# First stage of an encoder block in another order: one modulation summed on TensorE, two heads per output product

## The chip, the cores and the metric

The kernel runs on one core of one Trainium2 chip. The metric is the device time of one execution in microseconds (us), as the median of several runs. TensorE (PE in the profile) multiplies matrices and transposes through products with an identity; VectorE (DVE), ScalarE (ACT) and GpSimd (POOL) work on rows; SyncE (SP) issues the transfers. Each engine takes its own instructions strictly in order and waits on semaphores for the others.

## The reference

One encoder block on 512 tokens of 1024 channels, in float32. A mixing layer is followed by a layer of 16 experts.

```python
mod = silu(c) @ w_ada + b_ada
shift1, scale1, gate1, shift2, scale2, gate2 = split(mod, 6)
h = rms_norm(x, npm) * (1 + scale1) + shift1
q, k, v, zg = split(h @ w_in)               # 512, 128, 128, 1024 columns
attn = windowed_gqa(q, k, v, sink)          # 8 heads, 2 kv heads, band of +-128
u, vg = split(gelu(zg), 2)
gm = u * (W_s @ layer_norm(vg) + b_s)       # per chunk of 128 tokens, 8 groups
mix = concat([rms_norm(attn), rms_norm(gm)])
x = x + gate1 * rms_norm(mix @ w_out)
h2 = rms_norm(x, npf) * (1 + scale2) + shift2
y = experts(h2)       # each of 16 experts takes its best 64 tokens, SwiGLU, 2816 wide
x = x + gate2 * rms_norm(y)
```

## The kernel before

Two stages follow each other. The **first stage** is the mixing layer with the router; the **expert stage** streams the weights of 16 experts through 13 buffers of 1408 KB. The order in which the program writes its steps, and a scheduler that works at build time, fix the sequence on every engine; at run time nothing is reordered.

**Projection.** `SEQ` lists three kinds of step for the eight groups of 128 channels. `m` makes shift1 and scale1 of a group, `d` modulates the group (`modulate`, L332 to L334) into a high part `hh` and a low part `hl`, and `q` adds the group's products into q, k and v (`qkv`; every product is three, L346 to L348, with the weights split in parts `wh` and `wl`). A step `m` has two forms. For the groups in `MODPE` (0, 1, 2, 3, 5) TensorE sums 32 small products (`mod1_rows`, L293). For groups 4, 6 and 7 VectorE adds eight rows (`mod1_acc`, L315 and L317), and TensorE then sums over partitions (`mod1_cols`, L322).

**Gate units, up units.** Then come eight units `g` and eight units `u` of the gMLP's projection, 12 products each (`pg`, `pu`). For each unit GpSimd makes the low part of the weights (`wl`, L343). Into the gate units the kernel weaves the sums of gate1 and shift2 (`mod2(0)`, `mod2(1)`: eight VectorE instructions of 128x1024 on `racc` each, L553 and L555, with loads from `w_ada`); scale2 (`mod2(2)`, numbers in `M2`) and gate2 (`mod2(3)`, `M3`) lie in the attention steps. `mod2_cols` turns a finished sum into columns with TensorE (`pm`, then a transpose `pt`). `gate_norm` normalises one block of the gate values `vn`: statistics (L499), 1/sqrt, a scaling on VectorE (L505), and two products on GpSimd (L506, L507). Blocks 0 and 1 do so after the last units, blocks 2 and 3 in steps of the attention (`GN`).

**Attention steps.** A numbered loop of 26 steps follows. Step i makes the scores of one block and one pair of heads (`sp`, L430) and the softmax (L432 on), and two steps later transposes the probabilities (`ptr`, L454; copied to `pT`) and multiplies them with v (`po`, L462). Up units 4 to 7 are in steps 0 to 3. `todo` hangs the rest on step numbers: spatial gating, splitting the output weights (`wo`, `wz`, L654 and L657), the output projection (`py`), the residual (L698), the router's logits, and in step `RS` the ranks of the first three blocks (`rank_part`, L806). Step `GS` spreads gate2 over all partitions (L585).

**1/sqrt.** `rsqrt(dst, v, n)` guesses from the bits (L184), forms -v/2 (L186), and takes three Newton steps (L191 for n = 1, L193 and L194 for more, then L196). The norm of x is done in two calls, n = 3 and n = 1 (L258).

**Transfers.** All go out on SyncE's queue in program order. The expert weights are issued at L835, each into a buffer that an earlier tile has to leave.

Of the kernel before, what the change touches and what calls it, by code (L numbers as in the profile page):

```python
# [7 lines left out]
F32 = mybir.dt.float32  # L8
# [39 lines left out]
TINY = 2.0 ** -126  # L48


@with_exitstack
def encoder_block(ctx, tc, x, c, w_ada, b_ada, norm_pre_mix, norm_post_mix, w_in, sink, sgu_ln_g,
# [32 lines left out]
    # ---------------------------------------------------------------- loads  # L85
# [17 lines left out]
    # columns of w_ada for shift1, scale1 of 128 channels with the rows of w_in for q, k, v of these channels  # L103
# [18 lines left out]
    def more_loads():  # L122
# [15 lines left out]
        nc.sync.dma_start(lnb, sgu_ln_b.to_broadcast([P, DG]))  # L138
        wst = slot([NG, P], name="wst")
# [4 lines left out]
    # ---------------------------------------------------------------- constants  # L144
# [24 lines left out]
    def make_dist():  # L169
        """|distance|, or a huge number outside the window; keys in front of, of, behind the block"""  # L170
# [10 lines left out]
    def rsqrt(dst, v, n):  # L181
        """dst = 1/sqrt(v) for [P, n] f32, to f32's accuracy: a guess from the bits, then Newton."""
        i = rs.tile([P, n], I32, name="rs_i", tag=f"rs_i{min(n, 2)}", bufs=2 if n == 1 else 1)
        nc.vector.tensor_scalar(i, v.bitcast(I32), -0.5, float(0x5F3759DF), op0=OP.mult, op1=OP.add)  # L184
        h = rs.tile([P, n], F32, name="rs_h", tag=f"rs_h{min(n, 2)}", bufs=2 if n == 1 else 1)
        nc.vector.tensor_scalar(h, v, -0.5, None, op0=OP.mult)  # L186
        y = i.bitcast(F32)
        t = rs.tile([P, n], F32, name="rs_t", tag=f"rs_t{min(n, 2)}", bufs=2 if n == 1 else 1)
        for r in range(3):
# [5 lines left out]
            o = dst if r == 2 else rs.tile([P, n], F32, name="rs_y", tag=f"rs_y{min(n, 2)}")  # L195
            nc.vector.scalar_tensor_tensor(o, t, 1.5, y, op0=OP.add, op1=OP.mult)  # L196
            y = o
# [4 lines left out]
    def rms(src, n, junk, dst=None):  # L202
        """1/rms of the rows of src (one [P, n] or two halves of it)"""
        parts = src if isinstance(src, list) else [src]
        ss = rs.tile([P, len(parts)], F32, name="ss", tag=f"ss{len(parts)}")
        for i, p in enumerate(parts):
            sumsq(ss[:, i:i + 1], p, junk[:, :p.shape[1]])
        if len(parts) > 1:
            nc.vector.tensor_tensor(ss[:, 0:1], ss[:, 0:1], ss[:, 1:2], op=OP.add)
        v = rs.tile([P, 1], F32, name="vv")  # L210
        nc.vector.tensor_scalar(v, ss[:, 0:1], 1.0 / n, EPS, op0=OP.mult, op1=OP.add)
        r = rs.tile([P, 1], F32, name="rr", bufs=4) if dst is None else dst
        rsqrt(r, v, 1)
        return r

    # ---------------------------------------------------------------- parameters by column
# [20 lines left out]
    # ---------------------------------------------------------------- x: transposed; 1 / rms  # L237
# [18 lines left out]
    def x_rsqrt(b0, b1):  # L256
        v = ssx[:, b0:b1]
        nc.vector.tensor_scalar(v, v, 1.0 / D, EPS, op0=OP.mult, op1=OP.add)  # L258
# [8 lines left out]
    # ---------------------------------------------------------------- shift1, scale1; h  # L267
# [817 lines left out]
```

## Time and profile before

| | us |
|---|---|
| median of three runs | 1546.49 |
| lowest, highest | 1546.27, 1547.13 |
| span of the profiled execution | 1544.5 |
| TensorE busy | 1387.1 |
| VectorE busy | 429.7 |
| ScalarE busy | 188.9 |
| GpSimd busy | 116.0 |

The profile is one execution. Its span runs from the first to the last instruction; the page gives no other time of that execution, and the median is 2.0 us above the span. [...] The first sixth of the span and the rest have different limits, so a share over the whole says nothing on either of them.

### The profile page before, as it was taken

To read this page: it belongs to the slowest core of one execution; us is meant where nothing else is said; L and a number is where in the kernel's file an instruction comes from. 1 tells how busy PE (TensorE), PEld (TensorE's weight loads), DVE (VectorE), ACT (ScalarE), POOL (GpSimd) and SP (SyncE) were. 2 spreads that over 40 slices of the span, in tenths; PEclk is the share of its full clock that TensorE was granted. 3 is DMA by queue.
4 is the path that set the end of the run, shared out by engine and by line. 5 is a ranking of instruction groups with operands and counts; after the bars stand their busy time and mean duration, and the time that the engine had idled before them with its cause. 6 is when DMAs were issued, how large, how long until landed. Compare 5 with 4: busy or idle time off the path is not lost.

```text
span 1544.5 us, 17570 instructions
## 1 busy us (share of the span) xinstructions
PE 1387.1 (90%) x7282; PEld 619.8 (40%) x7282; DVE 429.7 (28%) x1087; ACT 188.9 (12%) x404; POOL 116.0 (8%) x144
## 2 busy tenths in 40 slices
PE   7888998999999998998898998989898989898986
PEld 5665665343444433333333333324242423333323
DVE  5789857112112120212112111112020303020104
ACT  3336433000010000000100000000000000000001
POOL 2457310000000000000000000000000000000002
PEclk9998999999999999999999999999999999999998
DMA  9776608999999999999999999999999999999995
GB/s 316 275 252 181 241 6 334 415 411 428 429 429 429 429 429 428 429 428 429 429 428 429 429 429 429 429 428 429 429 428 429 429 429 429 428 429 429 429 396 202
DMA packets 92711, 596.86 MB, mean 386 GB/s; under 512 B 8692, under 2 KB 31960, under 8 KB 44760
## 3 DMA queue, kind: packets, MB, share of 16 engines
q1 hardware_dynamic: 92632, 595.74, 93.3%
q8 instruction: 57, 0.93, 0.2%
q14 instruction: 22, 0.18, 0.0%
HBM read 593.62 MB, written 2.10 MB: 386 GB/s over the span
## 4 chain that ended last, share of the span: by engine, by line
DMA 60%; PE 28%; DVE 8%; issue 1%; ACT 1%; POOL 1%; SPq 0%; DVEq 0%; ACTq 0%; POOLq 0%
DMA w<-in_w_down_dram 23%; DMA w<-in_w_up_dram 19%; DMA w<-in_w_gate_dram 18%; PE pf L949 11%; PE pd L991 4%; PE px L888 1%; PE pys L1001 1%; PE py L348 1%; PE py L346 1%; PE po L462 1%; PE py L347 1%; DVE ex L851 1%; PE pd L1031 1%; DVE racc L555 1%; DVE acc L317 1%
## 5 line engine op out<-in xcount | busy, mean ns | idle before, releaser
L949 PE MATMUL pf<-w,ex 128*64 128x512 f32 (+1 forms) x3072 | 638.0, 561 | 42.0 <-DMA w<-in_w_up_dram 40.6
L949 PEld LDWEIGHTS pf<-w,ex 128*64 128x64 f32 x3072 | 215.0, 137 | 433.2 <-issue 326.2
L991 PE MATMUL pd<-w,ex 128*64 128x512 f32 (+1 forms) x1440 | 319.3, 563 | 33.7 <-DMA w<-in_w_down_dram 33.7
L991 PEld LDWEIGHTS pd<-w,ex 128*64 128x64 f32 x1440 | 109.9, 136 | 231.7 <-issue 126.0
L967 DVE TENSOR_TENSOR ex<-pf,ex 128x512 f32<-128x512 f32 (+1 forms) x48 | 30.4, 647 | 362.3 <-PE pf L949 362.0
L995 DVE TENSOR_SCALAR ex<-pd,gc 128x512 f32<-128x512 f32 x15 | 11.3, 751 | 377.6 <-PE pd L991 377.6
L907 POOL COPY ex<-ex 128x512 f32<-128x512 f32 x16 | 9.8, 613 | 1138.2 <-DVE ex L905 1058.0
L888 PE MATMUL px<-x_sb,ex 128*64 128x256 f32 x512 | 71.0, 386 | 8.6 <-DVE ex L864 7.4
L919 ACT ACTIVATE ex<-pot 128x512 f32<-128x512 f32 x16 | 9.6, 597 | 544.6 <-PE pot L917 544.6
L1007 DVE TENSOR_TENSOR y<-pys,y 128x512 f32<-128x512 f32 x112 | 68.2, 681 | 17.0 <-PE pys L1001 17.0
L974 ACT ACTIVATE ex<-pht 128x512 f32<-128x512 f32 (+1 forms) x48 | 23.5, 559 | 374.6 <-PE pht L973 374.6
L1001 PE MATMUL pys<-ex 64*128 64x512 f32 x240 | 55.6, 602 | 12.7 <-DVE ex L995 12.7
L900 DVE TENSOR_SCALAR ex<-pxt,mods 128x64 f32<-128x64 f32 x128 | 34.9, 337 | 92.0 <-PE pxt L895 92.0
L888 PEld LDWEIGHTS px<-x_sb,ex 128*64 128x64 f32 x512 | 41.3, 136 | 38.3 <-DVE ex L864 18.8
L851 DVE SCALAR_TENSOR_TENSOR ex<-rt,afs,before 128x512 f32<-128x512 f32 (+2 forms) x65 | 46.8, 719 | 12.3 <-PE rt L858 12.3
L913 DVE COPY gc<-pgc 128x1 f32<-128x1 f32 x16 | 2.5, 158 | 152.6 <-PE pgc L910 152.6
L555 DVE SCALAR_TENSOR_TENSOR racc<-ada,cs,racc 128x1024 f32<-128x1024 f32 x28 | 42.6, 1521 | 0.2
L959 ACT ACTIVATE ex<-pf 128x512 f32<-128x512 f32 (+1 forms) x48 | 26.9, 561 | 121.2 <-PE pf L949 120.4
L1001 PEld LDWEIGHTS pys<-ex 64*128 64x128 f32 x240 | 21.9, 186 | 47.1 <-DVE ex L995 25.9
L973 PE MATMUL pht<-ident,ex 128*128 128x128 f32 x176 | 25.7, 295 | 12.1 <-DVE ex L967 12.1
L973 PEld LDWEIGHTS pht<-ident,ex 128*128 128x128 f32 x176 | 22.7, 213 | 22.7 <-DVE ex L967 22.7
L890 ACT ACTIVATE ex<-px 128x256 f32<-128x256 f32 x32 | 12.3, 383 | 125.7 <-PE px L888 125.6
(254 smaller groups left out, 1086.3 us busy)
## 6 DMA issues: line engine op xcount, KB each, us to landing
w<-in_w_gate_dram SPq DMA_DIRECT2D x128, 1408.0 KB, 26.8
w<-in_w_up_dram SPq DMA_DIRECT2D x126, 1408.0 KB, 26.8
w<-in_w_down_dram SPq DMA_DIRECT2D x120, 1408.0 KB, 26.8
ada<-in_w_ada_dram SPq DMA_DIRECT2D x16, 1024.0 KB, 6.5
w<-in_w_down_dram SPq DMA_DIRECT2D x18, 512.0 KB, 9.6
wq<-in_w_ada_dram SPq DMA_DIRECT2D x16, 512.0 KB, 5.9
wi<-in_w_in_dram SPq DMA_DIRECT2D x4, 1024.0 KB, 5.2
wq<-in_w_in_dram SPq DMA_DIRECT2D x8, 384.0 KB, 6.2
```

The costliest lines, as they stand in the source:

```text
L555: nc.vector.scalar_tensor_tensor(acc[i], t[:, r], cs[:, k:k + 1], acc[i], op0=OP.mult, op1=OP.add)
L851: nc.vector.scalar_tensor_tensor(junk[:, :c1 - c0], p[:, c0:c1], afs[:, b, e:e + 1], before[:, o + c0:o + c1], op0=OP.subtract, op1=OP.is_ ...
L888: nc.tensor.matmul(px[i][h * CAP:(h + 1) * CAP, :256], ohr[:, b], x_sb[:, b, c0:c0 + 256], start=(b == 0), stop=(b == NB - 1))
L900: nc.vector.tensor_scalar(xs[:, k], pt[:, c0:c0 + CAP], s2[:, k:k + 1], sh2[:, k:k + 1], op0=OP.mult, op1=OP.add)
L949: nc.tensor.matmul(pb[n][h * 64:(h + 1) * 64, :NW[n]], XS[e][:, k], t, start=(i == 0), stop=(i == KD - 1))
L959: nc.scalar.activation(hid[:, n * 512:n * 512 + NW[n]], pg[n][:, :NW[n]], AF.Silu)
L967: nc.vector.tensor_tensor(hs, pu[n][:, :NW[n]], hs, op=OP.mult)
L973: nc.tensor.transpose(p[:, j * P:(j + 1) * P], hv[:, j0 + j], ident)
L974: nc.scalar.activation(hT[:, j0:j0 + n], p.rearrange("p (j t) -> p j t", j=4)[:, :n], AF.Copy)
L991: nc.tensor.matmul(pd[dh * 64:(dh + 1) * 64, c0:c0 + n], hT[:, j, h * CAP:(h + 1) * CAP], t[:, o - q * FF:o - q * FF + n], start=(h == 0 a ...
L1001: nc.tensor.matmul(p, OT[e][dh * 64:(dh + 1) * 64, b * P:(b + 1) * P], oe[dh * 64:(dh + 1) * 64, :], start=True, stop=True)
L1007: nc.vector.tensor_tensor(yb, p, yb, op=OP.add)
```

## The change

- All eight `m` steps go to TensorE; `mod1_acc` and `mod1_cols` with their 24 VectorE sums are gone.
- `mod2(0)` moves into `SEQ` as steps `a0` to `a3`; `mod2(1)` and `mod2(2)` take the gate units, with `mod2_cols` at gate unit 2 and up units 0 and 3. `M2` is gone; gate2 stays in the steps, numbers in `M3`.
- `gate_norm` runs once for four blocks after up unit 0, with one 1/sqrt.
- `rsqrt` takes -v/2 as its argument and makes a third-order step and one Newton step: six instructions where it were eight for n = 1, eight where it were eleven for n = 4. The norm of x is one call with n = 4.
- `attn_out` multiplies two pairs of heads at once: 256 columns where it were 128, in every second step. The last block's closing is split (0, 2), (2, 4).
- The loads of `wst` and of the first gate weights go out after other `q` steps.

```diff
-MODPE = (0, 1, 2, 3, 5)
-SEQ = "d0 m1 q0 d1 m2 d2 m3 q1 d3 m4 q2 d4 m5 q3 d5 m6 q4 d6 m7 q5 d7 q6 q7"
-M2 = (0, 0, 1, 1, 3)
-M3 = (8, 8, 9, 9, 10)
-GN = (None, None, 0, 0)
-GS, RS = 23, 21
+SEQ = "d0 m1 q0 d1 m2 d2 m3 q1 d3 m4 q2 d4 m5 q3 d5 m6 q4 d6 m7 a0 q5 d7 a1 q6 a2 q7 a3"
+M3 = (8, 8, 9, 9, 11)
+GS, RS = 20, 21
+ALPHA = (2 / 3) ** 0.2
+GUESS = 520466879.0
...
-        for r in range(3):
+
+        def square():
             if n == 1:
                 nc.vector.scalar_tensor_tensor(t, y, h, y, op0=OP.mult, op1=OP.mult)
             else:
                 nc.vector.tensor_tensor(t, y, y, op=OP.mult)
                 nc.vector.tensor_tensor(t, t, h, op=OP.mult)
...
+        square()
+        p = rs.tile([P, n], F32, name="rs_p", tag=f"rs_y{min(n, 2)}")
+        nc.vector.scalar_tensor_tensor(p, t, 5 / 3 / ALPHA ** 2, t, op0=OP.add, op1=OP.mult)
+        z = rs.tile([P, n], F32, name="rs_y", tag=f"rs_y{min(n, 2)}")
+        nc.vector.scalar_tensor_tensor(z, p, 1.25 / ALPHA ** 4, y, op0=OP.add, op1=OP.mult)
+        y = z
+        square()
+        nc.vector.scalar_tensor_tensor(dst, t, 1.5, y, op0=OP.add, op1=OP.mult)
...
-        for i in range(k1 - k0):
-            for g in range(2):
-                nc.tensor.matmul(po[n, j][g * HD:(g + 1) * HD, j * P:(j + 1) * P], v_sb[:, k0 + i, g * HD:(g + 1) * HD],
-                                 pT[g][:, i * P:(i + 1) * P], start=(i == 0), stop=(i == k1 - k0 - 1))
+        if j % 2:
+            for i in range(nk):
+                for g in range(2):
+                    nc.tensor.matmul(po[n, j][g * HD:(g + 1) * HD, (j - 1) * P:(j + 1) * P],
+                                     v_sb[:, k0 + i, g * HD:(g + 1) * HD], pTs[g][:, i].rearrange("p j q -> p (j q)"),
+                                     start=(i == 0), stop=(i == nk - 1))
...
-        mod2(k // 4, k % 4)
+        mod2(1 + k // 4, k % 4)
+        if k == 2:
+            mod2_cols(0)
...
-        if k < 2:
-            mod2_cols(k)
-        if GN[k] is None:
-            gate_norm(k)
...
+        if k in (0, 3):
+            mod2_cols(1 + k // 3)
+        if k == 0:
+            gate_norm()
```

What stands in a row on VectorE at the end of the projection, before (`qk` and `t` are copies of k and v out of the projection's last sums, `hl` is the last group's modulation, `racc` on `ada_770` to `ada_833` the sums of gate1):

```order
L334 SCALAR_TENSOR_TENSOR hl<-t_642,sh_160,hh 128x512
L405 COPY qk<-qkp 128x512
L410 COPY t_737<-qkp 128x512
L226 COPY pc_142<-pp 128x40
L553 TENSOR_SCALAR racc<-ada_770,cs 128x1024
L605 COPY v_sb<-pv 128x512
L555 SCALAR_TENSOR_TENSOR racc<-ada_770,cs,racc 128x1024
L555 SCALAR_TENSOR_TENSOR racc<-ada_793,cs,racc 128x1024 x2
L555 SCALAR_TENSOR_TENSOR racc<-ada_813,cs,racc 128x1024 x2
L555 SCALAR_TENSOR_TENSOR racc<-ada_833,cs,racc 128x1024 x2
```

And in the changed kernel:

```order
L305 SCALAR_TENSOR_TENSOR hl<-t_653,sh_160,hh 128x512
L353 TENSOR_SCALAR racc<-ada_622,cs 128x1024
L431 COPY qk<-qkp 128x512
L355 SCALAR_TENSOR_TENSOR racc<-ada_622,cs,racc 128x1024
L220 COPY pc_142<-pp 128x40
L436 COPY t_760<-qkp 128x512
L355 SCALAR_TENSOR_TENSOR racc<-ada_657,cs,racc 128x1024
L586 COPY v_sb<-pv 128x512
L355 SCALAR_TENSOR_TENSOR racc<-ada_657,cs,racc 128x1024
L355 SCALAR_TENSOR_TENSOR racc<-ada_689,cs,racc 128x1024 x2
L355 SCALAR_TENSOR_TENSOR racc<-ada_731,cs,racc 128x1024 x2
```

One of the eight gate1 sums has moved ahead of the copy of k out of the projection's sums; the other seven still stand behind that copy.

On GpSimd around the last splits of the up units, before (`wl` is a split, `vn` the normalised gate values, `pr` the probabilities):

```order
L343 TENSOR_TENSOR wl<-wi,wh 128x512 x14
L506 TENSOR_TENSOR vn<-vn,sgu 128x512
L507 TENSOR_TENSOR vn<-vn,sgu 128x512
L343 TENSOR_TENSOR wl<-wi,wh 128x512
L506 TENSOR_TENSOR vn<-vn,sgu 128x512
L507 TENSOR_TENSOR vn<-vn,sgu 128x512
L343 TENSOR_TENSOR wl<-wi,wh 128x512
L439 TENSOR_SCALAR pr<-pr,dn 128x256 x2
```

And in the changed kernel:

```order
L314 TENSOR_TENSOR wl<-wi,wh 128x512 x14
L540 TENSOR_TENSOR vn<-vn,sgu 128x512
L541 TENSOR_TENSOR vn<-vn,sgu 128x512
L540 TENSOR_TENSOR vn<-vn,sgu 128x512 x2
L541 TENSOR_TENSOR vn<-vn,sgu 128x512 x2
L314 TENSOR_TENSOR wl<-wi,wh 128x512
L540 TENSOR_TENSOR vn<-vn,sgu 128x512
L541 TENSOR_TENSOR vn<-vn,sgu 128x512
L314 TENSOR_TENSOR wl<-wi,wh 128x512
L465 TENSOR_SCALAR pr<-pr,dn 128x256 x2
```

The last split now stands behind eight products on `vn` where it stood behind four, and the last but one behind six where it stood behind two.

On TensorE around the attention's first scores, before (44 of the 96 products `pu` stand ahead of them, the other 52 between the scores of later steps):

```order
L278 MATMUL pm_1006<-racc,ones 32x256 x4
L346 MATMUL pu<-wh,hh 128x512
L347 MATMUL pu<-wl,hh 128x512
L348 MATMUL pu<-wh,hl 128x512
L285 MATMUL pt<-ident,rows_1011 128x128 x2
L430 MATMUL sp<-qk 128x256 x2
L346 MATMUL pu<-wh,hh 128x512
```

And in the changed kernel:

```order
L272 MATMUL pm_1087<-racc,ones 32x256 x4
L317 MATMUL pu<-wh,hh 128x512
L318 MATMUL pu<-wl,hh 128x512
L319 MATMUL pu<-wh,hl 128x512
L279 MATMUL pt<-ident,rows_1092 128x128 x2
L272 MATMUL pb<-wr,mods 32x16 x32
L456 MATMUL sp<-qk 128x256 x6
L317 MATMUL pu<-wh,hh 128x512
L318 MATMUL pu<-wl,hh 128x512
L319 MATMUL pu<-wh,hl 128x512
```

The sum `pm` ahead of the first scores was that of shift2 and is now that of scale2, and the scores of the first three steps stand together behind 93 of the 96 up products.

## Rows read from the trace of the kernel before

**Rows 1.** The page: its first line, and the chain that ended last.

```profile
span 1544.5 us, 17570 instructions
...
DMA 60%; PE 28%; DVE 8%; issue 1%; ACT 1%; POOL 1%; SPq 0%; DVEq 0%; ACTq 0%; POOLq 0%
```

**Rows 2.** SyncE's waits: what was waited for, us in total, times, longest.

```profile
SPq L835 <- PE py L348: 49.2, 2, 48.8
...
SPq L835 <- DVE ty L806: 15.9, 1, 15.9
```

**Rows 3.** Busy time from 110 to 120 us: PE, PEld, DVE, ACT, POOL, PEclk, DMA, GB/s.

```profile
110.00:120.00 10.00, 6.66 (x25) 3.56 (x25) 9.86 (x18) 1.72 (x5) 6.96 (x5) 0.66 0.71 236
```

**Rows 4.** TensorE's timeline, projection: start, us, instruction, [idle before <- releaser].

```profile
41.30 0.41 PE L322 MATMUL pm<-acc,ones 128*32 128x128 f32 x4 [1.90 <-DVE acc L317]
...
42.74 1.08 PE L293 MATMUL pm<-wq,cs 128*32 128x128 f32 x32
...
53.73 0.41 PE L322 MATMUL pm<-acc,ones 128*32 128x128 f32 x4 [2.59 <-DVE acc L317]
...
56.30 0.63 PE L348 MATMUL qkp<-hh,wl 128*128 128x512 f32 x1
...
69.64 0.39 PE L348 MATMUL qkp<-hh,wl 128*128 128x512 f32 x1
```

**Rows 5.** VectorE's timeline: the 1/sqrt of x's last block.

```profile
12.61 0.14 DVE L258 TENSOR_SCALAR ssx<-ssx 128x1 f32<-128x1 f32 x1
...
15.77 0.68 DVE L196 SCALAR_TENSOR_TENSOR rx<-rs_t,rs_y 128x1 f32<-128x1 f32 x1
```

**Rows 6.** VectorE's timeline, gate units and up units.

```profile
74.13 0.69 DVE L605 COPY v_sb<-pv 128x512 f32<-128x512 f32 x1 [2.34 <-PE pv L604]
74.73 13.73 DVE L555 SCALAR_TENSOR_TENSOR racc<-ada,cs,racc 128x1024 f32<-128x1024 f32 x7
93.56 1.29 DVE L499 BATCH_NORM_STATS2 st<-vn 128x6 f32<-128x512 f32 x2 [5.09 <-ACT vn L609]
...
108.36 1.27 DVE L555 SCALAR_TENSOR_TENSOR racc<-ada,cs,racc 128x1024 f32<-128x1024 f32 x1
```

**Rows 7.** GpSimd's timeline: a product on the gate values, twice.

```profile
108.52 2.23 POOL L506 TENSOR_TENSOR vn<-vn,sgu 128x512 f32<-128x512 f32 x1 [0.36 <-DMA ada<-in_w_ada_dram]
...
117.21 1.28 POOL L506 TENSOR_TENSOR vn<-vn,sgu 128x512 f32<-128x512 f32 x1 [2.88 <-DVE vn L505]
```

**Rows 8.** TensorE's timeline, attention's first five steps.

```profile
116.01 1.23 PE L430 MATMUL sp<-qk 64*128 64x256 f32 x4
...
130.93 0.70 PE L430 MATMUL sp<-qk 64*128 64x256 f32 x2
...
134.59 0.64 PE L278 MATMUL pm<-racc,ones 128*32 128x256 f32 x8
...
137.51 0.92 PE L430 MATMUL sp<-qk 64*128 64x384 f32 x4
```

**Rows 9.** VectorE's timeline: the first probabilities that wait behind the output weights' splits.

```profile
151.39 0.61 DVE L432 CUSTOM_DVE_ANT_0 pr<-sp,dist,nsink 128x384 f32<-128x384 f32 x1
```

**Rows 10.** TensorE's timeline, 206 to 266 us: products of 128 and of 256 columns; the tail.

```profile
206.35 0.43 PE L462 MATMUL po<-pT,v_sb 128*64 128x128 f32 x2 [0.17 <-ACT pT L459]
207.36 0.87 PE L462 MATMUL po<-pT,v_sb 128*64 128x128 f32 x10
...
252.83 1.93 PE L712 MATMUL ph<-ident,x_sb 128*128 128x128 f32 x8 [3.79 <-DVE x_sb L698]
...
258.25 2.03 PE L585 MATMUL spr<-ident,mods 128*128 128x128 f32 x16
...
261.63 4.06 PE L888 MATMUL px<-x_sb,ex 128*64 128x256 f32 x32 [1.24 <-DVE rank L872]
```

**Rows 11.** VectorE's timeline: first and last of the final 1/sqrt's eleven instructions.

```profile
1533.50 0.17 DVE L184 TENSOR_SCALAR rs_i<-vf 128x4 int32<-128x4 int32 x1
...
1535.29 0.16 DVE L196 SCALAR_TENSOR_TENSOR rf<-rs_t,rs_y 128x4 f32<-128x4 f32 x1
```

More of the change, by code (lines that the diff above doesn't have):

```diff
@@ L138, in more_loads, with load_wst @@
         nc.sync.dma_start(lnb, sgu_ln_b.to_broadcast([P, DG]))
+    def load_wst():
+        nonlocal wst
         wst = slot([NG, P], name="wst")
@@ L363, in qkv, with mod2 @@
             mm3(qkp[m], h[:, c0:c0 + P], l[:, c0:c0 + P], hh[k], hl[k], k == 0, k == KD - 1)
+    G0 = cp.tile([P, D], F32, name="G0")
+    mods = cp.tile([P, 4, 8], F32, name="mods")
+    g1c, sh2, s2, g2c = (mods[:, i] for i in range(4))
+    rb = cp.tile([P, NE], F32, name="rb")
+    acc = {}
+    def mod2(i, kk):
+        t = slot([2, D], name="ada2")
+        nc.sync.dma_start(t, ada[:, 2 * kk:2 * kk + 2, 2 + i])
+        if kk == 0:
+            acc[i] = (ea if i < 2 else at).tile([P, D], F32, name="racc")
+        for r in range(2):
+            k = 2 * kk + r
+            if k == 0:
+                nc.vector.tensor_scalar(acc[i], t[:, r], cs[:, k:k + 1], None, op0=OP.mult)
+            else:
+                nc.vector.scalar_tensor_tensor(acc[i], t[:, r], cs[:, k:k + 1], acc[i], op0=OP.mult, op1=OP.add)
@@ new lines, in mod2_cols @@
+    def mod2_cols(i):
+        pm = bank("pm2")
+        mod_rows(pm, ones, acc[i].rearrange("p (j w) -> p j w", j=4), 256, True, True)
+        rows = at.tile([P, 256], F32, name="rows2", tag="pT", bufs=2)
+        nc.vector.tensor_copy(rows, pm[:, :256])
+        m = mod_cols(rows, 256)
+        nc.vector.tensor_tensor(mods[:, i].rearrange("p (j q) -> p q j", j=4), m,
+                                pcol("ba", 16 + 8 * i, 8).rearrange("p (j q) -> p q j", j=4), op=OP.add)
+        if i == 0:
+            nc.vector.tensor_tensor(g1c, g1c, pcol("pom", 0, 8), op=OP.mult)
+            spread(G0, g1c)
+        elif i == 2:
+            nc.vector.tensor_tensor(s2, s2, pcol("npf", 0, 8), op=OP.mult)
+            pb = bank("pb")
+            for k in range(KD):
+                mod_rows(pb, sh2[:, k:k + 1], wr[:, k:k + 1].to_broadcast([P, 4, NE]), NE, k == 0, k == KD - 1)
+            nc.vector.tensor_scalar(rb, pb[:, :NE], -1.0, None, op0=OP.mult)
+            nc.vector.scalar_tensor_tensor(wsp[:, :, :NE], wr, -1.0, s2.unsqueeze(2).to_broadcast([P, KD, NE]),
+                                           op0=OP.mult, op1=OP.mult)
+        elif i == 3:
+            nc.vector.tensor_tensor(g2c, g2c, pcol("pof", 0, 8), op=OP.mult)
@@ L365, in encoder_block, with spread @@
+    def spread(dst, cols):
+        for i in range(2):
+            p = bank("spr")
+            for k in range(4):
+                kk = i * 4 + k
+                nc.tensor.matmul(p[:, k * P:(k + 1) * P], cols[:, kk:kk + 1].to_broadcast([P, P]), ident,
+                                 start=True, stop=True)
+            nc.scalar.activation(dst[:, i * 512:(i + 1) * 512], p, AF.Copy)
     for b in range(NB):
@@ L579, in spread @@
-    def spread(dst, cols):
-        for i in range(2):
-            p = bank("spr")
-            for k in range(4):
-                kk = i * 4 + k
-                nc.tensor.matmul(p[:, k * P:(k + 1) * P], cols[:, kk:kk + 1].to_broadcast([P, P]), ident,
-                                 start=True, stop=True)
-            nc.scalar.activation(dst[:, i * 512:(i + 1) * 512], p, AF.Copy)
     pacc = {}
```

166 lines of the change are left out of this document (48 added, 118 removed).

## The prediction

> **What bounds the kernel now.** Read the page first: a span of 1544.5 us, and a chain of work that ended last of which 60% is transfers [rows 1]. The chain's transfers are the expert weights, so from the first expert on the kernel runs at the pace at which weights arrive, and the changed stage lies ahead of that. It counts only by where it lets the transfers go on. SyncE's waits tell where it does not [rows 2]: once for 48.8 us, because buffers of expert weights are still held by the output weights that `py` reads, and once for 15.9 us on `ty`, which the ranks of the first expert write last. In both cases the queue stands still until the first stage moves on. So a microsecond that leaves the critical path of the first stage leaves the end, and one that is taken out beside it does not. I take this as one to one; little of it can be lost, since after the first expert there is no slack that an earlier start would only fill.
>
> The third view is the busy time of a stretch in the middle of the stage [rows 3]: from 110 to 120 us VectorE works 9.86 of 10 us, GpSimd 6.96, TensorE 6.66 at a mean granted clock of 0.66. There VectorE, not TensorE, is the engine on which the others wait. That is where the change works most.
>
> **Projection.** TensorE stood twice for the VectorE sums, 1.90 and 2.59 us [rows 4], together 4.5. After the second stop its products went at a clock of half: 0.63 us each where 0.39 is usual [rows 4]; by the distance of neighbours some seven products lost 0.2 us each, 1.4 in all, of which I count 1.2. Both go. In return three groups are now summed on TensorE: 32 small products take 1.08 us, where four took 0.41 [rows 4], so 0.7 us more each, 2.0. The 1/sqrt of x's last block ran from 12.61 to 16.45 [rows 5], two calls interleaved, 3.8 us. One call of eight dependent steps of 0.18 (from [rows 11]) and the scaling is 1.6, if nothing gets between; the bounds are 0.75 and 2.2 us earlier and I take 1.2. Sum: -4.5 - 1.2 - 1.2 + 2.0 = -4.9. The last product, which ended at 70.0 [rows 4], should end at about 65.2.
>
> The change says that gate1 is summed inside the projection. The order shows that only one of its eight instructions comes ahead of the copy that waits for the projection's end. The other seven stay behind it, as before.
>
> **Loads.** Four loads of gate1 and those of `wst` and the gate weights change places on SyncE's queue, into and within the projection. A load there waits for the buffer that an earlier step leaves; queued behind it are the next weights and, at the end, the first expert weights. In [rows 4] the stops were all named by VectorE sums and none by a transfer, and what goes out earlier in one place is gone in the next. I count zero, with 1 us against it if the weights of a group come late.
>
> **VectorE up to the gate values' scaling.** Seven sums took 13.73 us, 1.96 each [rows 6], because GpSimd works beside them; alone one takes 1.27 [rows 6]. Before, they and the copies ended at 88.5, that is 18.4 us after the projection. After, one sum (1.0 at least) is done earlier and the wait of 2.34 for v [rows 6] is filled with a sum: 65.2 + 18.4 - 3.3 = 80.3. Then come five sums of shift2, 5 x 1.96 = 9.8, to 90.1. The gate values, which came at 93.56 [rows 6], come by 4.8 us earlier, at 88.8, so VectorE has no wait for them (5.09 before). Then three more sums (5.9), four statistics (1.29 for two [rows 6], so 2.6) and their closings (1.0): 99.6. One 1/sqrt of eight short instructions (1.5), one sum of scale2 (1.96) and the first scaling (at most the 0.69 of a copy of its size [rows 6]) end at 103.8.
>
> **GpSimd's line of ten.** From here the order puts eight products on the gate values and the last two splits of the up units in a row. A product took 2.23 us beside a VectorE sum and 1.28 without [rows 7]. Bounds for ten: 12.8 and 22.3 us. VectorE has seven sums and three scalings left in this time, so I take eight at 2.23 and two at 1.28, 20.4: the last split ends at 124.2. Behind it TensorE has some seven products of the last up unit, 1.6 us at full clock and 3.0 at half (I take 2.1), and from the sum `pm` over the transposes and `pb` to the first scores 2.9 us, as from 134.59 to 137.51 before [rows 8]. The **first scores** stand at 129.2 us. Before they stood at 116.01 [rows 8]; attention now starts 13 us later, with nothing left to interleave.
>
> **What the later start costs.** Before, steps 0 to 3 shared VectorE with the eight sums of scale2 and two blocks of gate normalisation, and the fifth step's scores came 21.5 us after the first ones (137.51 against 116.01 [rows 8]). After, this work is done. What is left from the first to the fifth step is like the stretch from the fourth to the fifth, 6.6 us (130.93 to 137.51 [rows 8]), plus the extra scores of two earlier steps at about 0.7 each [rows 8], so 8.0. From the fifth scores to the probabilities that stand behind the output weights' splits it was 13.9 us (137.51 to 151.39 [rows 8, 9]), and nothing of that changes. The sums of gate2 stay in the steps, numbers 8, 9 and 11, behind this stretch. Sum: 129.2 + 21.9 = 151.1 where it was 151.39: -0.3. Two ends: if the line of ten goes at 1.28, TensorE's own work sets the first scores: 192 products of 512 columns at 0.25 us (twice the 0.127 of a record of 256 columns, [rows 10]) behind 65.2 are at 113.2, and the three modulations' columns and `pb` with a stretch at half clock add some 5, so 118, hence -11.5; if all ten take 2.23 and the products run at half clock, about 132, hence +2.7. So the long way round ends where it began, and what the first 100 us gained is spent in GpSimd's line.
>
> **Two heads per product.** One step's `po` instructions took 0.43 and 0.87 us in two pieces, 1.0 to 1.3 with what overlaps [rows 10], two steps 2.0 to 2.6. A pair takes as many instructions as one step, of 256 columns; the nearest row of 256 columns is `px`, 4.06 us for 32 records, 0.127 each [rows 10]. Twelve make 1.5. So 0.5 to 1.1 per pair, I take 0.8 for the four pairs with three key blocks, and 0.35 for two pairs with two that lie behind 151 us: 3.9 at best. TensorE isn't the last to arrive in each step, and I count 3.2 (ends 0 and 3.9). The copies move as much as before.
>
> **Tail and end.** Before the first expert, two 1/sqrt of n = 1 lie in series, each two instructions shorter at about 0.2: 0.4. The spread of gate2 (2.03 us [rows 10]) leaves the tail; before that TensorE waited 3.79 us for VectorE [rows 10], and there it can hide, but it was itself mostly beside the wait for the ranks (1.24 [rows 10]): 0 to 1.0, I take 0.5. The final 1/sqrt ran eleven instructions from 1533.50 to 1535.29 [rows 11], 0.18 each; three fewer are 0.55, bare on the path. Sum -1.45.
>
> **Sum.** -0.3 - 3.2 - 0.9 - 0.55 = -4.95. Against the profiled execution's 1544.5 that is a span of 1539.5; the median of the runs lies 2.0 above the span, so 1546.5 - 5.0 = **1541.5 us**.
>
> **Rivals.**
>
> *The hand-over is mild* (GpSimd's line mostly undisturbed). For it: 1.28 alone [rows 7], and VectorE may finish its sums before GpSimd's last four. The first scores come at 119 to 124, and the time is 1533 to 1537.
>
> *A wash.* The steps' softmax sets the pace behind 151 us, so that shorter `po` products are only waited for, and the line of ten is a little slower. The point of parity for the first scores alone is 129.5; with the savings behind them it is 134.1, the last split then ending at 129.1. Price of two neighbours that exclude each other fully: 1.27 [rows 6] + 1.28 [rows 7] = 2.55 us, the line 25.5, the last split at 129.3 and the first scores at 134.3: 1546.6. The measured 2.23 lies between 1.28 and 2.55; not all of the product's time was shared, so the trace does not exclude it. The Trainium skill, "SBUF — State Buffer", section "Who interferes with whom", says that the port pair which GpSimd shares with VectorE is an exclusive lock for a whole instruction, and that a VectorE instruction with two SBUF inputs contends with a GpSimd one that reads there. By that rule this rival would hold wherever the two alternate one by one; the 2.23 beside the 1.27 shows most of such a lock. The range of this rival is 1544 to 1548.
>
> *Slower: TensorE stands and wakes at half clock.* One place: the last two up units' splits stand behind the eight products on GpSimd. Six units done, TensorE has nothing else to do until these splits come, and it stops twice, for longer than the 2.59 us behind which its products took 0.63 instead of 0.39 [rows 4]; [rows 3] has a mean granted clock of 0.66 in such a stretch. The first scores then come at the upper bound of 132, and of the 21.9 us behind them some 9 are TensorE's own work (an estimate), which at 0.63 for 0.39 takes 5.5 more, bare, since up products no longer lie between: as if the first scores came at 137.5. Price 137.5 - 129.2 = 8.3, time 1549.8. It decides from a last split at about 129, where parity lies, and it is outside of what a measurement calls the same when the first scores count as at 137 or later.
>
> *The change doesn't do what it says*: gate1's sums mostly don't get into the projection. That is in the forecast already.
>
> **How the numbers follow.** Forecast, 1538 to 1543.5: 0.42. Mild: 0.18. Wash: 0.24. Slower: 0.16. 0.2% of this kernel, about what a measurement can tell from no change, is 3.1 us: faster means below 1543.4, slower above 1549.6. Faster gets forecast and mild, 0.60; of the wash all is same, 0.24; slower is 0.16. The range takes in the slower case's price of 1549.8 and the mild case down to its lower end; what it leaves out, the upper half of the slower case, the lowest part of the mild one and the far ends of the unknown costs, I put at 0.15: 1533 to 1550.5.
>
> **What would show it.** In the changed kernel's profile: the projection's last product ends near 65; no wait of TensorE on `acc` is there; VectorE's first scaling of the gate values ends near 104; GpSimd's last `wl` ends near 124; the first `sp` starts near 129, and the probabilities after the splits of the output weights near 151. If the first `sp` is below 124 the mild case holds, above 132 the slower one. The pairs of `po` show 0.13 us per record; if they do and the steps keep their distance, the wash holds. SyncE's wait on `py` ends some 4 us earlier than before, and the first expert's products start near 262. The forecast is wrong as a whole if an earlier start of the expert stage does not move the end one to one.

## The result, and the profile after

The changed kernel takes **1555.76 us** (median; 1554.35 to 1557.1), the kernel before 1546.49: a ratio of 1.0058 (95% interval 1.0046 to 1.0069). It is slower by 9 us where 5 us less were forecast, and outside of the range.

The page of the changed kernel gives its span and the chain (with [rows 1]), and the rate of transfers in 40 equal slices of the span:

```profile
span 1552.6 us, 17492 instructions
...
DMA  9965527999999999999999999999999999999995
GB/s 292 333 254 178 201 89 296 422 408 425 424 424 425 425 423 426 425 423 425 425 423 425 425 424 425 424 424 425 424 426 425 423 425 423 425 425 424 425 390 204
...
DMA 69%; PE 22%; DVE 4%; POOL 2%; ACT 1%; issue 1%; SPq 1%; DVEq 0%; ACTq 0%; POOLq 0%
```

The page of the kernel before has this line:

```profile
GB/s 316 275 252 181 241 6 334 415 411 428 429 429 429 429 429 428 429 428 429 429 428 429 429 429 429 429 428 429 429 428 429 429 429 429 428 429 429 429 396 202
```

This is the first thing to see. From the tenth slice to the third from last, where nothing but expert weights is moved, the rate is 423 to 426 GB/s where it was 428 or 429, all along. The bytes moved are the same 596.86 MB. One per cent of some 1270 us is 12 to 13 us.

Now the first stage. TensorE's timeline of the changed kernel (start, us, instruction, [idle before <- releaser]):

```profile
64.26 0.39 PE L319 MATMUL qkp<-hh,wl 128*128 128x512 f32 x1
...
116.64 0.80 PE L318 MATMUL pu<-wl,hh 128*128 128x512 f32 x1 [6.89 <-POOL wl L314]
123.28 0.50 PE L318 MATMUL pu<-wl,hh 128*128 128x512 f32 x1 [1.61 <-POOL wl L314]
...
126.97 1.57 PE L456 MATMUL sp<-qk 64*128 64x256 f32 x12
...
256.37 5.91 PE L866 MATMUL px<-x_sb,ex 128*64 128x256 f32 x32 [1.23 <-DVE rank L850]
...
263.12 19.11 PE L927 MATMUL pf<-w,ex 128*64 128x512 f32 x96
```

The last of these rows in the kernel before:

```profile
266.54 3.87 PE L949 MATMUL pf<-w,ex 128*64 128x512 f32 x18
```

VectorE's and GpSimd's timelines of the changed kernel:

```profile
69.70 8.83 DVE L355 SCALAR_TENSOR_TENSOR racc<-ada,cs,racc 128x1024 f32<-128x1024 f32 x5
...
91.51 0.70 DVE L531 BATCH_NORM_STATS2 st<-vn 128x6 f32<-128x512 f32 x1 [2.71 <-ACT vn L590]
...
101.80 0.54 DVE L539 TENSOR_SCALAR vn<-vn,mv,rln 128x512 f32<-128x512 f32 x1
...
148.60 0.60 DVE L458 CUSTOM_DVE_ANT_0 pr<-sp,dist,nsink 128x384 f32<-128x384 f32 x1
```

```profile
103.45 2.27 POOL L540 TENSOR_TENSOR vn<-vn,sgu 128x512 f32<-128x512 f32 x1
...
120.98 2.24 POOL L314 TENSOR_TENSOR wl<-wi,wh 128x512 fp32r<-128x512 f32 x1
```

Up to the probabilities the first stage went nearly as forecast, a little better; its end, in the last row, came 1 us later than forecast:

| step | forecast | changed kernel | before |
|---|---|---|---|
| last product of the projection ends | 65.2 | 64.7 | 70.0 [rows 4] |
| gate values there | 88.8 | 91.5 | 93.56 [rows 6] |
| first scaling of the gate values ends | 103.8 | 102.3 | - |
| GpSimd's line of ten, us | 20.4 | 19.8 | - |
| last split of the up units ends | 124.2 | 123.2 | - |
| first scores | 129.2 | 126.97 | 116.01 [rows 8] |
| probabilities after the splits | 151.1 | 148.60 | 151.39 [rows 9] |
| first expert's gather starts | - | 256.37 | 261.63 [rows 10] |
| first expert's first product | near 262 | 263.12 | 266.54 |

Each column is one execution. Of the changed kernel's order there are twelve more profiles, from the runs below that differ from it only in where the buffers stand. All thirteen put the end of the projection at 62.2 to 65.9, the first scores at 124.57 to 128.35, the probabilities at 146.18 to 151.92 and the first expert's product at 260.57 to 265.64, on average 263.8; the two profiles of the old order put that product at 266.54 and 265.50. So a difference of 1 or 2 us between two columns may be scatter.

In these two profiles the first stage hands over 3.4 us earlier. The rest of the span, from the first expert's first product to the end, is 1552.6 - 263.12 = 1289.5 us. Before it was 1544.5 - 266.54 = 1278.0. There, in a stage in which the change leaves the order of all work as it was, 11.5 us were lost.

### The profile page after: what moved, and what is told of

It is laid out like the page before. It is cut to its first block, busy times and chain, and to the rows that moved or that the text cites. A ratio compares the mean times of both kernels' runs of the same rounds, so it can differ in the third digit from the quotient of the medians.

```text
span 1552.6 us, 17492 instructions
## 1 busy us (share of the span) xinstructions
PE 1385.8 (89%) x7286; PEld 614.3 (40%) x7286; DVE 409.8 (26%) x997; ACT 185.4 (12%) x402; POOL 116.1 (7%) x144
## 2 busy tenths in 40 slices
DMA packets 92711, 596.86 MB, mean 384 GB/s; under 512 B 8692, under 2 KB 31960, under 8 KB 44760
## 4 chain that ended last, share of the span: by engine, by line
DMA 69%; PE 22%; DVE 4%; POOL 2%; ACT 1%; issue 1%; SPq 1%; DVEq 0%; ACTq 0%; POOLq 0%
DMA w<-in_w_down_dram 23%; DMA w<-in_w_up_dram 23%; DMA w<-in_w_gate_dram 23%; PE pf L927 7%; PE pd L969 2%; PE px L866 1%; PE po L492 1%; PE pd L1009 1%; PE py L317 1%; PE qkp L317 1%; PE py L319 1%; PE py L318 1%; PE qkp L318 1%; PE qkp L319 1%; PE pm L287 1%
## 5 line engine op out<-in xcount | busy, mean ns | idle before, releaser
L355 DVE SCALAR_TENSOR_TENSOR racc<-ada,cs,racc 128x1024 f32<-128x1024 f32 x28 | 48.2, 1723 | 0.4
L979 PEld LDWEIGHTS pys<-ex 64*128 64x128 f32 x240 | 21.9, 186 | 47.1 <-DVE ex L973 25.9
L314 POOL TENSOR_TENSOR wl<-wi,wh 128x512 fp32r<-128x512 f32 x16 | 26.2, 1639 | 22.4 <-ACT wh L313 22.4
```

Source lines behind the costliest of these rows:

```text
L355: nc.vector.scalar_tensor_tensor(acc[i], t[:, r], cs[:, k:k + 1], acc[i], op0=OP.mult, op1=OP.add)
L979: nc.tensor.matmul(p, OT[e][dh * 64:(dh + 1) * 64, b * P:(b + 1) * P], oe[dh * 64:(dh + 1) * 64, :], start=True, stop=True)
```

## The experiments

What differs in the expert stage can be read from the two built programs. The pool of small tiles (`rs`) became 128 bytes per partition shorter with the new 1/sqrt and its callers, from 2368 to 2240. The pools behind it moved down with it: the first of the 13 buffers for expert weights (11264 bytes per partition each) starts at byte 78848 of the partition before, a multiple of 512, and at 78720 after, 128 past a multiple of 256. Ten of the 13 buffers moved so: six of the first pool (`sl`), three of the second (`s2p`), one of the fourth (`s4p`). The three of the third pool (`s3p`) lie on the other side and stayed at 195552 on, 224 past a multiple of 256.

Theory A: this place sets the pace. Theory B: the streams are in another phase, since the first stage loads in another order. Theory C: the chip was slow, not the program.

**The changed kernel, buffers back in place**

```diff
     rs = ctx.enter_context(tc.tile_pool(name="rs", bufs=2))
+    nc.vector.memset(rs.tile([P, 32], F32, name="gap", bufs=1), 0.0)
     sl = ctx.enter_context(tc.tile_pool(name="sl", bufs=N1))
```

> The changed kernel with 128 bytes more in the pool of small tiles, so that ten of the 13 expert-weight buffers stand where they stood before the change (address 78848 on, a multiple of 512, instead of 78720 on); nothing else differs but one small memset at the start. Theory A (the place of the buffers sets the pace of the transfers): the expert stage goes at 429 GB/s again and the packets of 11264 bytes take 422 ns; time about 1543, that is 1546.5 less the 3.4 us by which the first stage of the changed kernel ended earlier (first expert product at 263.12 instead of 266.54). Theory B (the pace fell because the work and the transfers of the first stage stand in another order, so that the streams are in another phase): 424 to 425 GB/s as in the changed kernel, about 1555. Theory C (chip, not program): the kernel before, run beside it, is slow too.

Measured: 1542.38 us, ratio to the kernel before 0.9964 (0.9950 to 0.9978). In two more sets of runs: 1542.75 and 1541.79, ratios 0.9971 (0.9960 to 0.9983) and 0.9962 (0.9950 to 0.9974).

> The changed kernel with its ten weight buffers at multiples of 512 again, as the base for the two runs beside it on the same chip: 1542.4, some 5 us under the kernel before.

> The changed kernel with its ten weight buffers at multiples of 256, as the base for the run beside it: 1542.5.

The page of the first of the three:

```profile
span 1541.2 us, 17493 instructions
...
GB/s 321 343 226 171 205 92 283 409 410 429 428 428 429 429 428 428 428 428 429 429 428 428 429 429 429 429 428 428 429 429 429 428 429 428 428 430 428 429 396 204
```

The rate is back. What is left is the gain that was forecast, about 5 us: 5.2, 4.3 and 5.3 us below the kernel before in the same sets of runs.

**The kernel before, buffers 128 bytes lower**

```diff
-        ssf = rs.tile([P, 3, NB], F32, name="ssf")
+        ssf = rs.tile([P, 3, NB], F32, name="ssf", bufs=1)
...
-        v = rs.tile([P, NB], F32, name="vf")
+        v = rs.tile([P, NB], F32, name="vf", bufs=1)
...
-        r = rs.tile([P, NB], F32, name="rf")
+        r = rs.tile([P, NB], F32, name="rf", bufs=1)
```

> The kernel before, with three small tiles of the end held in one buffer each instead of two, which moves the same ten buffers 128 bytes down, to where they stand in the changed kernel; the order of all instructions stays. Theory A: about 1546.5 + 12 = 1558, 424 to 425 GB/s. Theory B and C: 1546.5, 429 GB/s.

Measured: 1556.87 us, ratio 1.0062 (1.0038 to 1.0086). Its page:

```profile
span 1555.0 us, 17570 instructions
...
GB/s 296 285 254 183 238 53 310 422 408 424 425 424 424 424 425 424 425 423 425 425 424 424 425 425 425 424 424 425 425 425 424 425 424 425 425 424 424 425 392 204
```

With not one instruction in another place, the kernel before loses what the changed kernel lost. Theories B and C fall; A is shown from both sides. Why the place sets the pace is another question, which these two runs don't answer.

**Which places are good**

> The changed kernel with the ten buffers another 128 bytes lower, 256 past a multiple of 512 instead of 384; the order of all instructions stays. Theory A with 512 bytes as the unit: as slow as the changed kernel or slower, 1554 to 1558. Theory A with 256 bytes as the unit: about 1543. Theory B: 1555.

The edit takes the three `bufs=1` above into the changed kernel. Measured: 1542.38, ratio 0.9970 (0.9958 to 0.9983). A multiple of 256 is enough.

> The changed kernel with the ten buffers at 64 past a multiple of 256 (address 78656 on), order unchanged. Theory A1 (whatever is not a multiple of 256 is slow): packets of 11264 bytes near 426 ns, 424 GB/s, 1555. Theory A2 (128 past a multiple of 256 is a special case; the three buffers at 224 past it never cost): 422 ns, 429 GB/s, 1542.

> The changed kernel with the ten buffers at 192 past a multiple of 256 (address 78784 on), order unchanged. After the run at 64 past (424 GB/s): if only multiples of 256 are fast, 424 GB/s and 1555; if the cost fell with the distance to the next multiple, between the two.

> The ten buffers at 224 past a multiple of 256 (address 78816 on), where the three others have always stood without showing a cost. If each buffer's own offset counts and 224 is a good one: 429 GB/s, 1542. If what counts is the offset of most of the buffers, or any offset but zero in these ten: 424 GB/s, 1555.

> The ten buffers at 32 past a multiple of 256 (address 78624 on). If only multiples of 256 are fast: 424 GB/s, 1555. If 32 is as harmless as 224 was in the three others: 429 GB/s, 1542.

These add 16, 48, 56 and 8 numbers of padding, as in the first diff, to the kernel at 256 past a multiple of 512. All four were slow: 1556.8, 1557.94, 1560.11 and 1559.55 us, one time each. With 128, none of the five offsets tried is harmless, and there is no slope between 64 and 192.

**The third pool**

```diff
+        if nch[0] - 1 == ORDER.index(2):
+            nc.gpsimd.memset(s3p.tile([P, 120], F32, name="gap3", bufs=1), 0.0)
```

> As the first, and the three buffers of the third pool, which stood at 480 bytes past a multiple of 512 in both kernels, are moved to a multiple of 512 too. Theory A in the form that each buffer's own offset counts: faster than the first, by up to 3/10 of the 12 us, so 1539 to 1543. Theory A in the form that these three never cost anything (packets of the kernel before took 422 ns whatever the buffer): the same as the first, about 1543. Theory B: 1555.

> The ten buffers at multiples of 256, the three others moved from 224 past to 128 past (address 195200 on). If each buffer's own offset counts and 128 is a bad one: 3/13 of the loss of 12 us, some 427 to 428 GB/s and 1545. If only the ten matter: 429 GB/s, 1542.5.

Measured, with all 13 at multiples of 256: 1542.31, ratio 0.9960 (0.9947 to 0.9972), no better than with ten. With the three at 128 past (88 numbers where the diff has 120): 1541.39, one time. With the ten at multiples of 256, these three cost nothing at any of the three places tried, so the first form of theory A, in which each buffer's offset counts by itself, is wrong.

**Six or four of the ten**

```diff
     sl = ctx.enter_context(tc.tile_pool(name="sl", bufs=N1))
+    gp = ctx.enter_context(tc.tile_pool(name="gp", bufs=1))
+    nc.vector.memset(gp.tile([P, 32], F32, name="gap"), 0.0)
```

The line moves the second and the fourth pool by 128 bytes: in the changed kernel to a multiple of 256, in the one at 256 past a multiple of 512 away from it.

> The changed kernel with the six buffers of the first pool at a multiple of 256 and four others (second and fourth pool) at 128 past one; the three of the third pool as ever; order unchanged. If every one of the ten counts for itself: 4/10 of the loss, some 427 GB/s and 1547. If the first pool alone counts: 429 GB/s and 1542. If one bad group spoils all: 424 GB/s and 1555.

> The reverse: the six buffers of the first pool at 128 past a multiple of 256, the four others at a multiple. If every one counts for itself: 6/10 of the loss, some 426 GB/s and 1550. If the first pool alone counts: 424 GB/s and 1555.

Measured: 1543.91 with four off, 1550.66 with six off, one time each. Busy times from 500 to 600 us (last column GB/s), four off and six off:

```profile
500.00:600.00 100.00, 93.66 (x479) 36.28 (x477) 15.41 (x40) 6.20 (x12) 0.61 (x1) 1.00 1.01 428
```

```profile
500.00:600.00 100.00, 93.66 (x486) 36.85 (x484) 16.43 (x42) 6.58 (x13) 0.61 (x1) 1.00 1.01 426
```

The clean measure is the part of the span behind the first expert's first product, since it leaves out how the first stage went:

| buffers off a multiple of 256 | rest of the span, us |
|---|---|
| none | 1277.1 |
| three of the third pool (224 past) | 1276.8 to 1278.9 in nine profiles; before 1278.0 |
| three of the third pool (128 past) | 1277.1 |
| these three and four others (128) | 1280.2 |
| these three and six others (128) | 1283.6 |
| these three and ten others (128) | 1289.5; the kernel before, so shifted, 1289.5 |
| the same at 64, 192 | 1290.1, 1290.6 |
| the same at 32, 224 | 1292.9, 1292.9 |

So the loss grows faster than the number of buffers: 0, some 2, 5 and 11.5 us for three, seven, nine and thirteen, where equal layouts differ by up to 2 us. The mean of all packets of 11264 bytes, which scatters less, says the same: 424.6 to 424.9 ns with none or three off, 425.7 with seven, 426.7 with nine, 428.8 with thirteen.

The packet records also show that a buffer's own place doesn't decide what its transfer costs. The buffers are filled in a fixed cycle: the six of the first pool, the three of the second, the three of the third, the one of the fourth. One can put the packets in the order of their starts and count them off by transfers, 128 packets each; at the borders that is not exact. Packets over 440 ns, 0.1% of them, are left out of these means. In the run with four of the ten off, the second pool's three transfers, off and right behind six into aligned buffers, took 422.0 to 422.2 ns a packet; the third pool's, off and behind those, 422.8, 425.4 and 426.2. In the kernel before, where they come behind nine into aligned buffers, the third pool's took 422.0, 422.2 and 422.3. So what a transfer loses depends on the transfers ahead of it, and three off behind nine aligned ones lose next to nothing. With six of the ten off, the third pool's three, behind only three aligned ones, took 422.6, 424.5 and 425.3. Why that is so stays open.

**One part of the change undone: pairs of heads**

```diff
-        if j % 2:
-            for i in range(nk):
...
+        for i in range(k1 - k0):
+            for g in range(2):
+                nc.tensor.matmul(po[n, j][g * HD:(g + 1) * HD, j * P:(j + 1) * P], v_sb[:, k0 + i, g * HD:(g + 1) * HD],
+                                 pT[g][:, i * P:(i + 1) * P], start=(i == 0), stop=(i == k1 - k0 - 1))
```

> The base with the output products of one pair of heads each, as before the change (and the last block's closing as before). The forecast counted 3.2 us for this part: 1545.6. Rival (the steps' softmax sets the pace, the shorter products are only waited for): within 0.5 us of the base.

Measured: 1546.09, ratio 0.9987 (0.9974 to 0.9999), against 1542.75 of its base: 3.3 us for this part, where 3.2 were counted. The scatter of the single runs leaves 1.8 to 5.7 us for it (95%), so the close agreement means little; that the part gains more than the rival's 0.5 is what the run shows. Two steps of one pair each, then one product of two pairs in the base:

```profile
205.73 0.43 PE L489 MATMUL po<-pT,v_sb 128*64 128x128 f32 x2 [0.17 <-ACT pT L486]
206.53 0.87 PE L489 MATMUL po<-pT,v_sb 128*64 128x128 f32 x10
...
211.71 0.43 PE L489 MATMUL po<-pT,v_sb 128*64 128x128 f32 x2 [0.29 <-ACT pT L486]
212.90 0.87 PE L489 MATMUL po<-pT,v_sb 128*64 128x128 f32 x10
```

```profile
211.59 0.65 PE L493 MATMUL po<-pT,v_sb 128*64 128x256 f32 x2 [0.67 <-ACT pT L489]
212.88 1.51 PE L493 MATMUL po<-pT,v_sb 128*64 128x256 f32 x10
```

The entries themselves add up to 2.60 and 2.16: 0.44 us a pair, where the forecast counted 0.8, and ten records of 256 columns took 1.51, that is 0.15 each and not 0.13. That the rest of the 3.3 lies in the switches and waits, now half as many, is likely but not shown.

**One part undone: 1/sqrt**

> The base with 1/sqrt of as many instructions as before the change (guess, one more small instruction, three Newton steps: 8 for n = 1, 11 for n = 4), the same calls otherwise. The forecast counted 0.4 in the tail, 0.55 at the end and some 1 at the start and at the gate values: 1543.5 to 1544.5. Rival (they lie beside other work, all but the last): 0.55, 1543.

```diff
+        h2 = rs.tile([P, n], F32, name="rs_h", tag=f"rs_h{min(n, 2)}", bufs=2 if n == 1 else 1)
+        nc.vector.tensor_scalar(h2, h, 1.0, None, op0=OP.mult)
...
+        for r in range(3):
```

Measured: 1550.16, ratio 1.0023 (1.0013 to 1.0032), 7.4 us above its base. Both expectations were far too low. The run is no clean price of the instructions, since the scheduler put others in another order too, but the trace shows where it begins. VectorE's norm of x and TensorE's first and last products of the projection, first with the old 1/sqrt, then the base:

```profile
16.67 0.15 DVE L198 SCALAR_TENSOR_TENSOR rx<-rs_t,rs_y 128x4 f32<-128x4 f32 x1
```

```profile
21.39 0.77 PE L311 MATMUL qkp<-hh,wh 128*128 128x512 f32 x1
21.97 0.63 PE L312 MATMUL qkp<-hl,wh 128*128 128x512 f32 x1
...
66.89 0.39 PE L313 MATMUL qkp<-hh,wl 128*128 128x512 f32 x1
```

```profile
14.76 0.16 DVE L206 SCALAR_TENSOR_TENSOR rx<-rs_t,rs_y 128x4 f32<-128x4 f32 x1
```

```profile
19.27 0.47 PE L318 MATMUL qkp<-hh,wh 128*128 128x512 f32 x1
19.58 0.40 PE L319 MATMUL qkp<-hl,wh 128*128 128x512 f32 x1
...
62.61 0.39 PE L320 MATMUL qkp<-hh,wl 128*128 128x512 f32 x1
```

The norm of x comes 1.9 us later, TensorE starts 2.1 us later and at half clock (0.63 us a product where the base has 0.40), and the projection ends 4.3 us later. Not all of that is the old 1/sqrt's. The thirteen profiles of the changed order start the projection's products at 18.46 to 20.30 and end them at 62.2 to 65.9, so 1.1 and 1.4 us lie beyond their scatter; and in five of the thirteen, the changed kernel's own among them, a product of 0.63 us is among the first four too. The first scores come at 132.21, at least 3.9 us behind the thirteen, so a part arises after the projection. How much of the 7.4 us is the price of the instructions and how much that of the other order stays open.

**Parts alone, in the old order**

> The kernel before with two parts of the change alone, two heads per product and the third-order 1/sqrt; its order of modulations and gate normalisation, its VectorE sums and its two calls for the norm of x stay, the ten buffers at multiples of 256 (the last quarter of the gate2 sums is closed at step 11 as in the changed kernel). By the measured 3.3 us of the pairs and a forecast of 1.5 to 2 for 1/sqrt: 1546.5 - 5 = 1541.5. If the new order gains by itself (-0.3 by the forecast, and up to -2 with the projection): no faster than the base at 1542.4. If it costs (the late first scores): about 1540 or less, faster than the base.

Measured: 1547.57, ratio 0.9991 (0.9977 to 1.0004): no gain at all, where 5 us were expected. VectorE's timeline shows where a part of it went:

```profile
148.69 0.60 DVE L427 CUSTOM_DVE_ANT_0 pr<-sp,dist,nsink 128x384 f32<-128x384 f32 x1
...
149.22 5.09 DVE L657 SCALAR_TENSOR_TENSOR wz<-wo,pc,wz 128x1024 fp32r<-128x1024 f32 x4
154.23 0.61 DVE L427 CUSTOM_DVE_ANT_0 pr<-sp,dist,nsink 128x384 f32<-128x384 f32 x1
```

The scheduler now puts one of the two softmax instructions of a step ahead of the output weights' splits and the other behind them, where it starts at 154.23; before both stood behind them, from 151.39 [rows 9], the second here:

```profile
151.92 0.61 DVE L432 CUSTOM_DVE_ANT_0 pr<-sp,dist,nsink 128x384 f32<-128x384 f32 x1
```

That is 2.3 us later. It was not tried whether the gain comes back when both stand together again.

> The kernel of the run before this one, with all eight first modulations on TensorE too and one call for the norm of x; gate1's sums and the gate normalisation still where they stood before the change. The projection should end some 5 us earlier (65 instead of 70). If that reaches the end: 1536 to 1537. If VectorE, which is busy from 70 to 152 us, gives it back: down to 1540, with the first scores near 112 instead of 116.

```diff
-MODPE = (0, 1, 2, 3, 5)
+MODPE = tuple(range(8))
...
-            x_rsqrt(b, NB)
+            x_rsqrt(0, NB)
...
-        if b == NB - 2:
-            x_rsqrt(0, b + 1)
```

Measured: 1542.73, ratio 0.9959 (0.9941 to 0.9978), as fast as the whole change with its buffers in place, and 2.7 us behind the slower of the two times expected. Its first scores came at 110.88, near the 112 expected and not at some 127, and it ended no earlier: that the new order of gate1's sums and the gate normalisation by itself is worth next to nothing agrees with the forecast's -0.3.

**Gate2's spread**

> The base with gate2's spread in step 23 again, as before the change, instead of step 20: it stands right ahead of the first expert's gather products. In the changed kernel these took 5.91 us at a mean granted clock of 0.59; before the change, and in the run with the old order and the new projection, where the spread's 2.03 us stood ahead of them, 4.06 at 1.00. If the spread keeps the clock up and hides in the wait for the ranks: 4.06 again, the time 1.9 us below the base. If it only delays: the time equal to the base or up to 1 us above.

```diff
-GS, RS = 20, 21
+GS, RS = 23, 21
```

In the changed kernel the spread's 2.03 us have gone from the tail, and TensorE's granted clock fell there. Busy times around the first expert's gather (before PEclk, then DMA share, GB/s), first before the change and then after:

```profile
261.00:266.00 5.00, 4.37 (x34) 2.73 (x34) 2.96 (x16) 0.65 (x2) 0.61 (x1) 1.00 0.99 408
```

```profile
256.00:262.00 6.00, 5.63 (x32) 3.73 (x32) 2.68 (x14) 0.39 (x1) 0.61 (x1) 0.59 1.00 414
```

At 0.59 the gather took 5.91 us where it had taken 4.06 at 1.00 [rows 10]: 1.9 of the 5.3 us by which it started earlier were lost at once. With the spread back in its old step:

```profile
254.80 3.76 PE L386 MATMUL spr<-ident,mods 128*128 128x128 f32 x16
...
259.91 4.06 PE L867 MATMUL px<-x_sb,ex 128*64 128x256 f32 x32 [1.24 <-DVE rank L851]
```

Measured: 1543.12, ratio 0.9971 (0.9960 to 0.9981), beside 1541.79 of its base; the expected 1.9 us didn't come. The gather took 4.06 again, but the spread went at half clock itself (3.76) and the ranks waited for it. So the spread, put there, costs about what the slow clock did.

## Why the prediction was wrong

**The step that failed is in the first paragraph**: "It counts only by where it lets the transfers go on", and with it "I take this as one to one; little of it can be lost". The sum has no term for the expert stage's own time; without a reason it was put at no change. That time grew by 11.5 us, from 1278.0 to 1289.5. The hand-over itself did go one to one: with the ten buffers back at multiples of 256, the rest of the span was 1276.8 to 1278.9 us, whether the first expert's product came at 260.57 or at 270.86. The loss was put as a matter of slack. The expert stage has none, as said, and that is why one per cent on its transfers came out in full. I had counted what the change does to the order, and not that a change in the number and size of tiles in a pool moves the buffers behind it. No row of the trace before shows where a buffer stands. Its place does stand in the built program, and the changed program could have been looked at for it.

**What was right.** With the ten buffers back at multiples of 256 the changed kernel takes 1541.8 to 1542.75 us in three sets of runs, where 1541.5 was forecast. The forecast's case, not the mild one and not the wash, is what the first stage did.

That the sum came out so close is in part luck. In the two profiles the later start gave 2.5 us more than counted, and from the probabilities to the first expert's product the changed kernel gained only 0.6 us (2.8 to 3.4) where the pairs and the tail were to give 4.1. The slow gather took 1.9 of these; where the other 1.6 are was not found. Hand-over and end together make 3.8 us in these profiles, while the medians of the three sets say 4.3 to 5.3.

Projection: -4.9 counted, -5.3 measured (70.0 to 64.7). The loads that changed places, counted at zero, show no cost in it.

VectorE: the sums ended at 78.5, not 80.3, so the gate values were last to arrive and VectorE waited 2.71 us for them. The step "so VectorE has no wait for them" was wrong by that; the scaling came 1.5 us early all the same.

GpSimd's line: 20.4 counted, 19.8 measured; its products took at most 2.27 us beside VectorE, not the 2.55 of the wash's full exclusion. TensorE stood 6.89 and 1.61 us for the two splits.

Later start: -0.3 counted, -2.8 measured (151.39 to 148.60), mostly since the first scores came 2.2 us earlier than counted. By the averages of the thirteen profiles and the two of the old order it is 2.3 (151.8 to 149.5). The upper end of this term was added up wrongly: 132 + 21.9 is 153.9, which makes +2.5 and not +2.7.

Pairs of heads: 3.2 counted, 3.3 measured, known to 1.8 to 5.7 only. The products themselves gave about half of what was counted for a pair (0.44 for 0.8), so the agreement is in part luck too.

Tail: -0.9 counted, with the spread's removal as a gain of 0.5. That term was wrong: the gather behind it fell to a mean granted clock of 0.59 and gave 1.9 us back, and putting the spread back gained nothing either.

End: 0.55 counted, 0.41 measured, from 1.95 [rows 11] to 1.54 us, start of the first instruction to end of the last; eight now follow each other at 0.20 where eleven did at 0.18. VectorE's timeline of the changed kernel:

```profile
1541.97 0.17 DVE L187 TENSOR_SCALAR rs_i<-vf 128x4 int32<-128x4 int32 x1
...
1543.35 0.16 DVE L205 SCALAR_TENSOR_TENSOR rf<-rs_t,rs_y 128x4 f32<-128x4 f32 x1
```

**The rivals.** The slower case was forecast with another cause, a late GpSimd line; its price did not arise (first scores at 126.97, not at 132 or later). That the sign came out as in that rival says nothing for it.

## What to carry to other kernels

Where a stage is bound by streaming into buffers, a change elsewhere that resizes a pool in front of them can move these buffers and cost more than it gains. Look at the buffers' start addresses in the built program, pad the pool so that they fall on multiples of 256 bytes, and only then measure what the change itself does. In the trace the sign is a rate of transfer that is lower by one per cent in a stage whose order didn't change. Here three unaligned buffers among ten aligned ones cost nothing that could be seen; with all 13 unaligned it was 11.5 us.

## What the runs showed of the hardware

With ten of the 13 buffers (and the other three) off a multiple of 256 bytes in a partition, the transfers moved 423.4 to 424.5 GB/s on average over the slices from the tenth to the third from last; with the ten at multiples, 428.5 to 428.8. With four or six of the ten off they moved 427.7 and 426.5. The packets of 11264 bytes, by the trace's packet records, took 422 ns each in nearly all cases with the ten aligned, 424.6 to 424.9 on average; in the changed kernel most took 424 to 433, 428.8 on average. Packets of 512 bytes in the first stage went from 27.4 to 31.6 ns on average. They followed the first pool: 31.3 with its six buffers off alone, 27.4 with the four others off alone.

The Trainium skill, "DMA: Bandwidth & Descriptors", section "How a descriptor splits into AXI transactions", says that a descriptor is split into transactions of 256 bytes that must start at multiples of 256. It says so of reading; whether it holds for the place that a transfer writes to, it doesn't say. If it does, 11264 bytes off such a multiple make 45 transactions where aligned ones make 44, an estimate of 2% in transactions from the Trainium skill's rule; the runs show 1% in time, the same direction. The Trainium skill also counts the wasted bytes, by which, as an estimate, 192 past should cost three times what 64 past does; the runs show 1290.6 and 1290.1 us, no difference. And the three buffers of the third pool, which by the Trainium skill's rule should cost too, cost nothing here as long as the ten others were aligned.
